# A one-layer streaming encoder: natural projections in 512-column stripes, weights in a ring, tokens in half pieces

## The chip, the core and the metric

The kernel runs on one core of one Trainium2 chip. The metric is the device time of one execution in microseconds. The core has a matrix engine (TensorE, PE in the profile, with its weight loads as PEld), VectorE (DVE), ScalarE (ACT), GpSimd (POOL) and SyncE (SP), whose queue issues all of this kernel's transfers. Each engine works through its own queue in order; semaphores join them.

## The reference, cut to what matters

One layer over 16 meta tokens and 2048 prompt tokens, and over 8 streams of 16 new tokens, in float32. All projections of a layer are columns of one weight matrix `w_in` of 1024 x 8280:

```
h  = layer_norm(tokens)
(g_q, g_k, g_v, g_low, g_r, d_q, d_k, d_v, i_q, i_k, i_w, d_z, m_a, m_b) = split(h @ w_in)
A) log_f = log_sigmoid(g_low @ gla_w2 + b) / 16 ; S_t = diag(exp(log_f)) S_{t-1} + k^T v ; o = q S
   y_a = (rms_norm(o) * g * silu(g_r)) @ w_gla                       # linear attention, 4 heads
B) I[t,s] = sum_h w[t,h] relu(q_idx[t,h] . k_idx[s]) ; keep the best 256 keys of each token
   y_b = (softmax attention over the kept keys * silu(d_z)) @ w_dsa  # 16 heads, 4 key heads
out = layer_norm(ALPHA * h + (sigmoid(m_a + .) * y_a + sigmoid(m_b + .) * y_b) @ w_out)
```

New keys, values, indexer keys and recurrence states are returned too.

## The kernel before, in words

A matrix product in float32 is made of three: each operand is split into a high part and the rest, and `mm3` (L265 to L267) multiplies high by high, high by low and low by high, for eight blocks k of 128 rows, 24 matmuls in all, into one PSUM tile.

The 17 tiles of 128 tokens and the 16 meta tokens form six pieces of up to 384 columns. `phase_keys` normalizes each tile, transposes it into x (`xh`, `xl`, 8 blocks by 384 columns each) and computes keys, values and the indexer's keys from two sets of 300 weight columns. Then `project(g)` runs for three groups of two pieces: [4, 5], [2, 3], [0, 1]. The x of the first group stays from `phase_keys`; that of the others is read back from `d_xt` and split again. A stripe is a set of weight columns: `weights` loads it from `w_in` in pieces (`raw`), ScalarE casts each to its high part `whi`, GpSimd subtracts for `wlo` (L144). A transposed stripe (`stripe_t`, `tsp`) has the weights stationary and passes 272 or 384 token columns; a natural stripe (`natural`, `nat`) has 128 tokens stationary and passes the weights. gv, gr and z are natural, in 256 columns. Results are evicted through tiles of the pool `ev` and stored to scratch in DRAM.

Between the stripes of a group stand the indexer's blocks (`index_block`: scores, relu on ScalarE, weighted sum on VectorE), and `select`, a search on VectorE for each token's threshold that makes the masks of the kept keys. It is put 2500 instructions later than written, so that it runs beside the projections.

`phase2` runs the attention `attend(j)` for j from 15 down. Between its steps stands the side work: the gates of the linear attention (`gla_gates`), the sample streams' attention, their linear attention, then 16 chunks. 13 steps of it are put 1500 instructions earlier than written, so that they can run beside the last projections. The output projections follow (`gla_project`, `finish`).

The order on every engine is written out by a scheduler that simulates the program when it is built: of the instructions that are ready it takes the one written first, moved by the shifts above. A tile takes a place of its pool, and waits until the tile that had that place, or that had the same bytes in an earlier pool, is read for the last time. Pools lie on a stack from the left and one from the right. From the left stand, in `phase1`, after a constant: kp, scp, iqp, tk, jk, then xp0, xp1, xp2 (24 KB a partition each), ev, ws. In `phase2` stand there kdu0, kdu1, stu, gi, gt, gm, gc, sb. The side work's large tiles are in sb: three places under the tag `s4`, of 4.25 KB, and two of `kn`, of 2 KB. A chunk of the gates has two tiles `x` and two `e` there. Three x pools are handed out by the list `slots`; the last group has xp2 and xp1. In the last stripe of the second group the pieces are taken in reverse (`flip`).

Lines used below: L144 `tt`, L156 `act`, L159 the cast in `split_sb`, L256 the weight DMAs, L445 and L446 the indexer's matmuls, L596 the x loads, L611 the natural stores, L682 the gates' matmul, L1192 the sample attention's scores, L1129 to L1133 attention's scores and maxima.

Of the kernel before, what the change touches and what calls it, by code (L numbers as in the profile page):

```python
# [21 lines left out]
P = 128  # L22
# [31 lines left out]
VLATE = 60  # L54
PIECE = 720
# [64 lines left out]
class Trunk:  # L120
    def __init__(self, tc, i, o):
        self.tc, self.nc, self.i, self.o = tc, tc.nc, i, o
        self.turn = 0
        self.spare = self.flip = False
# [115 lines left out]
    def weights(self, parts, pool=None, name="", eng=None):  # L240

        nc = self.nc
        width = sum(n for _, n in parts)
        w = self.i["w_in"][0].rearrange("(k p) c -> p k c", p=P)
        if pool is None:
            hi = self.ws.tile([P, KT, width], F32R, name="whi")
            lo = self.ws.tile([P, KT, width], F32R, name="wlo")
        else:
            hi = pool.tile([P, KT, width], F32R, name="whi" + name, tag="sc")
            lo = pool.tile([P, KT, width], F32R, name="wlo" + name, tag="sc")  # L250
# [23 lines left out]
    def prep_x(self, t, xh, xl, c, keep):  # L274
# [9 lines left out]
        for q in range(2):  # L284
            ps = self.pi.tile([P, 4, P], F32, name="pt", tag="pi")
            for k in range(4):
                kk = 4 * q + k
                nc.tensor.transpose(ps[:, k, :r], h[:r, kk * P : (kk + 1) * P], self.ident[:r, :r])
            s = slice(4 * q, 4 * q + 4)
            self.split(xh[:, s, c : c + r], xl[:, s, c : c + r], ps[:, :, :r])  # L290
            if keep is not None:
                f = self.ev.tile([P, 4, P], F32, name="xf", tag="ev")
                nc.scalar.copy(f[:, :, :r], ps[:, :, :r])
                nc.sync.dma_start(keep[:, s, c : c + r], f[:, :, :r])

    def nat(self, x, c, r, w):

        ps = self.pp.tile([P, 512], F32, name="pp")
        (hi, lo), (xh, xl) = w, x
        n = hi.shape[-1]  # L300
        self.mm3(ps[:r, :n], lambda k: xh[:, k, c : c + r], lambda k: xl[:, k, c : c + r],
                 lambda k: hi[:, k, :], lambda k: lo[:, k, :], KT)
        return ps[:r, :n]

    def tsp(self, x, c, n, w, a):

        ps = self.pp.tile([P, 512], F32, name="pp")
        (hi, lo), (xh, xl) = w, x
        self.mm3(ps[:, :n], lambda k: hi[:, k, a : a + P], lambda k: lo[:, k, a : a + P],
                 lambda k: xh[:, k, c : c + n], lambda k: xl[:, k, c : c + n], KT)  # L310
        return ps[:, :n]

    def keys(self, t, x, c, w1, w2):
# [13 lines left out]
        xi = self.ev.tile([P, 80], F32, name="xi", tag="evs", bufs=4)  # L327
# [16 lines left out]
        xd = self.ev.tile([P, 2, 64], F32, name="xd", tag="evs", bufs=4)  # L344
# [8 lines left out]
        gl = self.ev.tile([16, P], F32, name="gl", tag="evs", bufs=4)  # L353
# [32 lines left out]
    def xtiles(self):  # L386
        q = self.slots.pop(0)
        return [self.xp[q].tile([P, KT, PMAX], F32R, name="x" + n) for n in "hl"]

    def stripe_t(self, g, c0, width, meta, evac):  # L390
        w = self.weights([(c0, width)])
        for q in GROUPS[g][:: -1 if self.flip else 1]:
# [167 lines left out]
    def phase1(self):  # L560
        nc, tc, i = self.nc, self.tc, self.i
        with ExitStack() as c:
# [7 lines left out]
            self.xp = [c.enter_context(tc.tile_pool(name=f"xp{q}", bufs=1)) for q in range(3)]  # L570
            self.ev = c.enter_context(tc.tile_pool(name="ev", bufs=4))
# [8 lines left out]
            self.x, self.slots = {}, [0, 1, 2, 0, 1, 2, 0, 1, 2, 1]  # L580
# [7 lines left out]
    def project(self, g):  # L588
        nc = self.nc
        for q in GROUPS[g]:  # L590
            if q not in self.x:
                self.x[q] = xh, xl = self.xtiles()
                n = PCN[q]
                for k in range(0, KT, 2):
                    raw = self.raw(n)
                    nc.sync.dma_start(raw, self.d["xt"][q][:, k : k + 2, :])  # L596
                    self.split_sb(xh[:, k : k + 2, :n], xl[:, k : k + 2, :n], raw)
# [4 lines left out]
        def natural(col, dst, base, meta, evac):  # L602
            w = self.weights([(col, 256)])
            for t, q in tiles:
# [5 lines left out]
                evac(e[:r, :256], ps)  # L610
                nc.sync.dma_start(self.d[dst][COL[t] : COL[t] + r, col - base : col - base + 256], e[:r, :256])  # L611
# [4 lines left out]
        def silu_norm(e, ps):  # L616
            self.act(e, ps, AF.Silu)
            self.tt(e, e, self.gng[:], OP.mult, eng=nc.gpsimd)
# [5 lines left out]
            "gv": (4, lambda c: natural(C_GV + c, "gv", C_GV, True, self.copy)),  # L624
            "q": (4, lambda c: st(g, C_DQ + c, 256, False, self.ev_heads)),
            "gr": (4, lambda c: natural(C_GR + c, "gr", C_GR, False, silu_norm)),
            "z": (4, lambda c: natural(C_DZ + c, "z", C_DZ, False, silu)),
# [4 lines left out]
        def step(n, c):  # L632

            self.spare = g == len(GROUPS) - 1 and n in SPARE

            self.flip = g == len(GROUPS) - 2 and (n, c) == (order[-1], 256 * (kinds[n][0] - 1))
            kinds[n][1](c)
            self.spare = self.flip = False

        steps = [lambda n=n, c=256 * q: step(n, c) for n in order for q in range(kinds[n][0])]  # L640
# [849 lines left out]
```

## Time and profile before

| | us |
|---|---|
| median of 3 runs (3590.15 to 3598.61) | 3597.57 |
| the profiled execution's own time | 3593.96 |
| its span | 3592.2 |
| TensorE busy | 3483.6 |
| VectorE busy | 2528.4 |
| ScalarE busy | 1450.9 |
| GpSimd busy | 1088.8 |

Busy times are sums over the whole span, which has stages with different limits: keys to about 200 us, projections to about 1860 us, attention with side work, and the output stage from about 3190 us. A matmul's recorded time runs until its last column is out and covers part of the next matmul's; how dense TensorE works is seen from the times between starts, or from the weight loads.

### The profile page before, as it was taken

To read this page: it belongs to the slowest core of one execution; us is meant where nothing else is said; L and a number is where in the kernel's file an instruction comes from. 1 tells how busy PE (TensorE), PEld (TensorE's weight loads), DVE (VectorE), ACT (ScalarE), POOL (GpSimd) and SP (SyncE) were. 2 spreads that over 40 slices of the span, in tenths; PEclk is the share of its full clock that TensorE was granted. 3 is DMA by queue.
4 is the path that set the end of the run, shared out by engine and by line. 5 is a ranking of instruction groups with operands and counts; after the bars stand their busy time and mean duration, and the time that the engine had idled before them with its cause. 6 is when DMAs were issued, how large, how long until landed. Compare 5 with 4: busy or idle time off the path is not lost. (4 is left out here: it accounts for less than half of the span.)

```text
span 3592.2 us, 66024 instructions
## 1 busy us (share of the span) xinstructions
PE 3483.6 (97%) x24196; PEld 3212.5 (89%) x24196; DVE 2528.4 (70%) x5813; ACT 1450.9 (40%) x3092; POOL 1088.8 (30%) x1412
## 2 busy tenths in 40 slices
PE   7999999999999998999999999999999999989999
PEld 6999999999999998998887788888877888879998
DVE  7737998799999998964436677676765666544444
ACT  4435223433324323322535556566565344331110
POOL 3122242242342334434411345455410000022221
PEclk9999999999999999999999999999999999999999
DMA  8642443254442345445573433333343345564431
GB/s 265 202 131 82 139 121 108 83 157 127 119 145 73 103 134 148 140 134 159 171 199 94 122 109 97 102 105 99 100 121 88 89 120 135 151 192 136 124 115 62
DMA packets 550340, 457.77 MB, mean 127 GB/s; under 512 B 95248, under 2 KB 522528, under 8 KB 550016
## 3 DMA queue, kind: packets, MB, share of 16 engines
q1 hardware_dynamic: 550016, 453.56, 43.9%
q8 instruction: 190, 3.11, 0.4%
q14 instruction: 134, 1.10, 0.1%
HBM read 292.49 MB, written 160.92 MB: 126 GB/s over the span
## 5 line engine op out<-in xcount | busy, mean ns | idle before, releaser
L144 POOL TENSOR_TENSOR wlo<-raw,whi 128x512 fp32r<-128x512 f32 x360 | 482.3, 1360 | 817.1 <-ACT whi L159 706.7
L150 DVE TENSOR_SCALAR_CACHE_REDUCE junk<-sc,cand 128x272 bf16<-128x272 f32 (+6 forms) x512 | 701.6, 1370 | 16.9
L265 PE MATMUL pp<-whi,xh 128*128 128x256 f32 (+3 forms) x1952 | 562.1, 288 | 3.5 <-ACT whi L159 2.3
L265 PE MATMUL pp<-xh,whi 128*128 128x384 f32 (+2 forms) x1728 | 563.6, 326 | 1.9 <-ACT whi L159 1.1
L267 PE MATMUL pp<-whi,xl 128*128 128x256 f32 (+3 forms) x1952 | 560.8, 288 | 4.4 <-DVE xl L144 4.4
L267 PE MATMUL pp<-xh,wlo 128*128 128x384 f32 (+2 forms) x1728 | 563.0, 327 | 1.0 <-POOL wlo L144 1.0
L266 PE MATMUL pp<-xl,whi 128*128 128x384 f32 (+2 forms) x1728 | 563.4, 326 | 0.0
L266 PE MATMUL pp<-wlo,xh 128*128 128x256 f32 (+3 forms) x1952 | 561.9, 288 | 0.0
L265 PEld LDWEIGHTS pp<-whi,xh 128*128 128x128 f32 (+1 forms) x1952 | 371.9, 191 | 12.7 <-issue 4.3
L267 PEld LDWEIGHTS pp<-whi,xl 128*128 128x128 f32 (+1 forms) x1952 | 371.0, 190 | 11.3 <-DVE xl L144 6.9
L266 PEld LDWEIGHTS pp<-wlo,xh 128*128 128x128 f32 (+1 forms) x1952 | 371.5, 190 | 7.8 <-issue 5.2
L1131 DVE CUSTOM_DVE_ANT_0 lgl<-pl,mkl 128x348 f32<-128x348 f32 (+8 forms) x608 | 296.1, 510 | 102.8 <-PE pl L1130 65.8
L265 PE MATMUL pd<-xh,wh 128*128 128x242 f32 (+3 forms) x1152 | 327.7, 285 | 8.2 <-ACT wh L1347 4.5
L159 ACT CAST whi<-raw 128x512 fp32r<-128x512 f32 (+1 forms) x344 | 199.2, 622 | 319.7 <-DMA raw<-in_w_in 204.8
L265 PEld LDWEIGHTS pp<-xh,whi 128*128 128x128 f32 x1728 | 325.1, 188 | 3.3 <-ACT whi L159 1.7
L267 PEld LDWEIGHTS pp<-xh,wlo 128*128 128x128 f32 x1728 | 324.8, 188 | 2.5 <-POOL wlo L144 1.8
L266 PE MATMUL pd<-xl,wh 128*128 128x242 f32 (+3 forms) x1152 | 324.6, 282 | 2.1 <-DVE xl L144 2.1
L266 PEld LDWEIGHTS pp<-xl,whi 128*128 128x128 f32 x1728 | 325.1, 188 | 0.6
L267 PE MATMUL pd<-xh,wl 128*128 128x242 f32 (+3 forms) x1152 | 324.5, 282 | 0.8 <-POOL wl L144 0.8
L156 ACT ACTIVATE lgl<-lgl,mx 128x1040 f32<-128x1040 f32 (+7 forms) x256 | 249.9, 976 | 177.9 <-DVE mx L1133 171.4
L1129 PE MATMUL pl<-kd,q 128*128 128x348 f32 (+14 forms) x800 | 302.5, 381 | 14.1 <-DVE mx L1131 4.9
L1130 PE MATMUL pl<-kd,q 128*128 128x348 f32 (+14 forms) x800 | 261.7, 330 | 0.0
(252 smaller groups left out, 7592.7 us busy)
## 6 DMA issues: line engine op xcount, KB each, us to landing
raw<-in_w_in SPq DMA_DIRECT2D x360, 256.0 KB, 3.2
q<-d_q SPq DMA_DIRECT2D x272, 128.0 KB, 3.0
d_h<-x SPq DMA_DIRECT2D x17, 512.0 KB, 3.3
d_gv<-en SPq DMA_DIRECT2D x68, 128.0 KB, 1.9
d_gr<-en SPq DMA_DIRECT2D x68, 128.0 KB, 2.0
d_z<-en SPq DMA_DIRECT2D x68, 128.0 KB, 1.7
v<-d_gv SPq DMA_DIRECT2D x17, 512.0 KB, 3.7
gr<-d_gr SPq DMA_DIRECT2D x17, 512.0 KB, 3.6
```

The costliest lines, as they stand in the source:

```text
L144: (eng or self.nc.vector).tensor_tensor(out, a, b, op=op)
L150: (eng or self.nc.vector).tensor_scalar(out, a, s1, s2, op0=op0, op1=op1, **kw)
L156: self.nc.scalar.activation(out, a, f, **kw)
L159: (self.nc.vector.tensor_copy if self.spare else self.nc.scalar.copy)(out, src)
L265: mm(ps, ah(k), bh(k), start=k == 0, stop=False)
L266: mm(ps, ah(k), bl(k), start=False, stop=False)
L267: mm(ps, al(k), bh(k), start=False, stop=k == n - 1)
L1129: nc.tensor.matmul(ps[:, :m], q[:, u, :], kd, start=True, stop=False)
L1130: nc.tensor.matmul(ps[:, :m], q[:, 2 + u, :], kd, start=False, stop=True)
L1131: nc.vector.tensor_tensor_reduce(lg[z1][:, a : a + m], ps[:, :m], mk[z1][:, a : a + m], 1.0, NEG, OP.add, OP.max, mx[:, s : s + 1])
```

## The change

Natural stripes have 512 columns. The weight tiles `whi` and `wlo` of 8 blocks become rings of six places each, every place 1024 elements a partition: four blocks of a 256-column stripe or two of a 512-column one; `weights` now returns two functions of k. Raw pieces hold two blocks up to 384 columns and one of 512, in four places instead of three. x is kept in halves of four blocks, each half in one of five pools taken in turn, and `slots` and `flip` are gone. The pool ev has six places instead of four, its small tiles eight instead of four. The area that the program reserves for dynamic DMAs at the foot of every partition is 1 KB instead of 16 KB.

```diff
+DMA_SCRATCH = 1024
+RING = 6
+RAWB = 4
...
     def raw(self, n):
-        t = self.ws.tile([P, 2 * PMAX], F32, name="raw", bufs=3)
-        return t[:, : 2 * n].rearrange("p (k c) -> p k c", k=2)
+        t = self.ws.tile([P, 2 * PMAX], F32, name="raw", bufs=RAWB)
+        two = 2 if n <= PMAX else 1
+        return t[:, : two * n].rearrange("p (k c) -> p k c", k=two)
...
     def weights(self, parts, pool=None, name="", eng=None):
...
-        if pool is None:
-            hi = self.ws.tile([P, KT, width], F32R, name="whi")
-            lo = self.ws.tile([P, KT, width], F32R, name="wlo")
...
-        for q in range(4):
-            s = slice(2 * q, 2 * q + 2)
-            raw = self.raw(width)
-            a = 0
-            for c, n in parts:
-                nc.sync.dma_start(raw[:, :, a : a + n], w[:, s, c : c + n])
-                a += n
-            self.split_sb(hi[:, s, :], lo[:, s, :], raw, eng)
-        return hi, lo
+        each = 1024 // width if pool is None else KT
+        hi, lo = [], []
+        for q in range(0, KT, each):
+            for x, name in (hi, "whi"), (lo, "wlo"):
+                if pool is None:
+                    t = self.ws.tile([P, 1024], F32R, name=name, bufs=RING)
+                    x.append(t[:].rearrange("p (k c) -> p k c", c=width))
+                else:
+                    x.append(pool.tile([P, KT, width], F32R, name=name + str(width), tag="sc"))
+            two = 2 if 2 * width <= 2 * PMAX else 1
+            for k in range(0, each, two):
+                raw = self.raw(width)[:, :two]
+                a = 0
+                for c, n in parts:
+                    nc.sync.dma_start(raw[:, :, a : a + n], w[:, q + k : q + k + two, c : c + n])
+                    a += n
+                self.split_sb(hi[-1][:, k : k + two, :], lo[-1][:, k : k + two, :], raw, eng)
+        return (lambda k: hi[k // each][:, k % each, :]), (lambda k: lo[k // each][:, k % each, :]), width
...
     def xtiles(self):
-        q = self.slots.pop(0)
-        return [self.xp[q].tile([P, KT, PMAX], F32R, name="x" + n) for n in "hl"]
+
+        halves = []
+        for _ in range(2):
+            self.xp.append(self.xp.pop(0))
+            halves.append([self.xp[-1].tile([P, 4, PMAX], F32R, name="x" + n) for n in "hl"])
+        return list(zip(*halves))
...
-            self.xp = [c.enter_context(tc.tile_pool(name=f"xp{q}", bufs=1)) for q in range(3)]
-            self.ev = c.enter_context(tc.tile_pool(name="ev", bufs=4))
+            self.xp = [c.enter_context(tc.tile_pool(name=f"xp{q}", bufs=1)) for q in range(5)]
+            self.ev = c.enter_context(tc.tile_pool(name="ev", bufs=6))
...
         def natural(col, dst, base, meta, evac):
-            w = self.weights([(col, 256)])
+            w = self.weights([(col, 512)])
...
                 e = self.ev.tile([P, 512], F32, name="en", tag="ev")
-                evac(e[:r, :256], ps)
-                nc.sync.dma_start(self.d[dst][COL[t] : COL[t] + r, col - base : col - base + 256], e[:r, :256])
+                evac(e[:r], ps)
+                nc.sync.dma_start(self.d[dst][COL[t] : COL[t] + r, col - base : col - base + 512], e[:r])
...
-            "gv": (4, lambda c: natural(C_GV + c, "gv", C_GV, True, self.copy)),
+            "gv": (2, lambda c: natural(C_GV + c, "gv", C_GV, True, self.copy)),
...
-            self.flip = g == len(GROUPS) - 2 and (n, c) == (order[-1], 256 * (kinds[n][0] - 1))
...
-    nc = bacc.Bacc("TRN2", target_bir_lowering=False, num_devices=1)
+    nc = bacc.Bacc("TRN2", target_bir_lowering=False, num_devices=1, dynamic_dma_scratch_size=DMA_SCRATCH)
```

gr and z go from four stripes to two in the same way.

## Rows read from the trace of the kernel before

**Rows 1.** The page, parts 1 and 2: busy us of TensorE; its granted clock by slice.

```profile
PE 3483.6 (97%) x24196; PEld 3212.5 (89%) x24196; DVE 2528.4 (70%) x5813; ACT 1450.9 (40%) x3092; POOL 1088.8 (30%) x1412
PEclk9999999999999999999999999999999999999999
```

**Rows 2.** Windows: stretch, length, busy us (xinstructions) by engine, clock, DMA share, GB/s.

```profile
core 0: us, PE busy (x) PEld busy (x) DVE busy (x) ACT busy (x) POOL busy (x), PEclk, DMA share, GB/s
0.00:200.00 200.00, 175.73 (x1231) 168.06 (x1231) 140.15 (x301) 83.92 (x245) 48.61 (x52) 0.98 0.72 218
200.00:1600.00 1400.00, 1379.50 (x9380) 1368.35 (x9380) 1235.02 (x1984) 502.61 (x1040) 484.02 (x402) 1.00 0.42 121
1600.00:1860.00 260.00, 254.99 (x1719) 234.36 (x1718) 100.14 (x197) 101.34 (x163) 91.62 (x63) 0.98 0.60 171
1860.00:2640.00 780.00, 757.28 (x5198) 625.94 (x5200) 535.60 (x1894) 455.35 (x976) 330.35 (x642) 0.99 0.39 107
2640.00:3190.00 550.00, 526.20 (x4171) 459.78 (x4165) 330.80 (x1109) 246.36 (x540) 46.10 (x160) 0.99 0.45 121
3190.00:3592.20 402.20, 389.85 (x2505) 356.06 (x2505) 186.68 (x330) 61.34 (x129) 88.07 (x95) 0.99 0.40 124
```

**Rows 3.** Timeline of TensorE, 499 to 509 us: two of 80 matmuls, 76 starts apart.

```profile
499.93 0.28 PE L265 MATMUL pp<-whi,xh 128*128 128x256 f32 x1
509.05 0.28 PE L266 MATMUL pp<-wlo,xh 128*128 128x256 f32 x1
```

**Rows 4.** Timeline of TensorE, output stage: two of 44 matmuls, 42 starts apart.

```profile
3573.94 0.39 PE L265 MATMUL fo<-woh,mgh 128*128 128x512 f32 x1
3583.46 0.39 PE L265 MATMUL fo<-woh,mgh 128*128 128x512 f32 x1
```

**Rows 5.** Tile whi on TensorE: min/median/max ns, first and last start us.

```profile
L265 PE MATMUL pp<-whi,xh x1952: 274/283/617, 13.5 to 1749.5; 128*128 128x256 f32 x163, 128*128 128x300 f32 x28, 128*16 128x256 f32 x4, 128*16 128x300 f32 x1
L266 PE MATMUL pp<-xl,whi x1728: 276/334/522, 179.5 to 1858.5; 128*128 128x384 f32 x161, 128*128 128x256 f32 x28, 128*128 128x272 f32 x3
```

**Rows 6.** Groups by shape, 200 to 1860 us, ScalarE and GpSimd: count, busy, mean ns, idle before.

```profile
L159 ACT CAST whi<-raw 128x512 fp32r<-128x512 f32 x325 | 187.0, 620 | 302.5 <-DMA raw<-in_w_in 191.4 <-PE pp L266 108.5 <-issue 1.7
L144 POOL TENSOR_TENSOR wlo<-raw,whi 128x512 fp32r<-128x512 f32 x351 | 469.4, 1357 | 789.0 <-ACT whi L159 678.5 <-DVE whi L159 20.2 <-PE pi L446 18.9
L144 POOL TENSOR_TENSOR xl<-raw,xh 128x768 fp32r<-128x768 f32 x12 | 21.9, 1848 | 25.6 <-ACT xh L159 25.6
```

**Rows 7.** Waits of TensorE, 100 to 1860 us: us, times, longest.

```profile
PE pi L445 <- ACT rl L156: 18.8, 14, 4.2
PE pp L265 <- ACT whi L159: 1.1, 2, 0.6
```

**Rows 8.** The page, part 3: DMA queues, packets, MB, share.

```profile
q1 hardware_dynamic: 550016, 453.56, 43.9%
q8 instruction: 190, 3.11, 0.4%
q14 instruction: 134, 1.10, 0.1%
```

**Rows 9.** Tile d_xt: loads of x pieces, us from issue to landing.

```profile
DMA to landing us min/median/max: 2.5/3.7/4.9
```

**Rows 10.** Windows of tile pg alone (TensorE, its loads, VectorE, ScalarE).

```profile
1600.00:1860.00 260.00, 46.19 (x202) 26.70 (x202) 26.09 (x48) 22.86 (x43) 0.98 0.60 171
```

**Rows 11.** Windows of tile ge alone (VectorE, ScalarE, GpSimd).

```profile
1600.00:1860.00 260.00, 27.96 (x24) 31.04 (x40) 20.56 (x10) 0.98 0.60 171
```

**Rows 12.** Groups of ScalarE, 1600 to 1860 us.

```profile
L156 ACT ACT_TABLE_LOAD x21 | 26.9, 1283 | 0.4
```

**Rows 13.** Tiles gl and ks on TensorE: first and last start us.

```profile
L682 PE MATMUL pg<-gl,w x40: 374/587/692, 1673.3 to 1747.3; 16*128 16x512 f32 x24, 16*128 16x400 f32 x8, 16*128 16x256 f32 x8
L1192 PE MATMUL pg<-ks,qsh x32: 282/287/428, 1757.7 to 1918.2; 128*128 128x272 f32 x32
```

More of the change, by code (lines that the diff above doesn't have):

```diff
@@ L123, in __init__ @@
         self.turn = 0
-        self.spare = self.flip = False
+        self.spare = False
     @contextmanager
@@ L289, in prep_x @@
             s = slice(4 * q, 4 * q + 4)
-            self.split(xh[:, s, c : c + r], xl[:, s, c : c + r], ps[:, :, :r])
+            self.split(xh[q][:, :, c : c + r], xl[q][:, :, c : c + r], ps[:, :, :r])
             if keep is not None:
@@ L326, in keys @@
         nc.sync.dma_start(d["v"][c0 : c0 + r, :], vt[:r])
-        xi = self.ev.tile([P, 80], F32, name="xi", tag="evs", bufs=4)
+        xi = self.ev.tile([P, 80], F32, name="xi", tag="evs", bufs=8)
         nc.scalar.copy(xi[:r, 0:64], p2[:, 212:276])
@@ L343, in keys @@
         self.stt(xi[:r, 0:64], xi[:r, 0:64], mu, self.ing[:r], OP.subtract, OP.mult)
-        xd = self.ev.tile([P, 2, 64], F32, name="xd", tag="evs", bufs=4)
+        xd = self.ev.tile([P, 2, 64], F32, name="xd", tag="evs", bufs=8)
         for q in range(2):
@@ L352, in keys @@
         self.split(self.kih[:, kc : kc + r], self.kil[:, kc : kc + r], ps[:, 0, :r])
-        gl = self.ev.tile([16, P], F32, name="gl", tag="evs", bufs=4)
+        gl = self.ev.tile([16, P], F32, name="gl", tag="evs", bufs=8)
         nc.scalar.copy(gl[:, :r], ps[:16, 1, :r])
@@ L386, in xtiles @@
     def xtiles(self):
-        q = self.slots.pop(0)
-        return [self.xp[q].tile([P, KT, PMAX], F32R, name="x" + n) for n in "hl"]
+        halves = []
[3 more added lines that the diff above has]
+        return list(zip(*halves))
     def stripe_t(self, g, c0, width, meta, evac):
         w = self.weights([(c0, width)])
-        for q in GROUPS[g][:: -1 if self.flip else 1]:
+        for q in GROUPS[g]:
             s = META if q == 0 and not meta else 0
@@ L596, in project @@
                     nc.sync.dma_start(raw, self.d["xt"][q][:, k : k + 2, :])
-                    self.split_sb(xh[:, k : k + 2, :n], xl[:, k : k + 2, :n], raw)
+                    r = slice(k % 4, k % 4 + 2)
+                    self.split_sb(xh[k // 4][:, r, :n], xl[k // 4][:, r, :n], raw)
         tiles = [(t, q) for q in GROUPS[g] for t in PIECES[q]]
@@ L623, in project @@
             "gk": (2, lambda c: st(g, C_GK + c, 256, True, self.ev_act("gk", C_GK, AF.Copy))),
[L624 removed]
+            "gv": (2, lambda c: natural(C_GV + c, "gv", C_GV, True, self.copy)),
             "q": (4, lambda c: st(g, C_DQ + c, 256, False, self.ev_heads)),
[L626 to L627 removed]
+            "gr": (2, lambda c: natural(C_GR + c, "gr", C_GR, False, silu_norm)),
+            "z": (2, lambda c: natural(C_DZ + c, "z", C_DZ, False, silu)),
             "ma": (4, lambda c: st(g, C_MA + c, 256, False, self.ev_act("ma", C_MA, AF.Sigmoid, biascol=0))),
@@ L634, in step @@
             self.spare = g == len(GROUPS) - 1 and n in SPARE
-            self.flip = g == len(GROUPS) - 2 and (n, c) == (order[-1], 256 * (kinds[n][0] - 1))
             kinds[n][1](c)
-            self.spare = self.flip = False
-        steps = [lambda n=n, c=256 * q: step(n, c) for n in order for q in range(kinds[n][0])]
+            self.spare = False
+        wide = "gv", "gr", "z"
+        steps = [lambda n=n, c=(512 if n in wide else 256) * q: step(n, c) for n in order for q in range(kinds[n][0])]
         blocks = [t for t, _ in tiles if t not in ("m", "s", 0)]
```

20 lines of the change are left out of this document (8 added, 12 removed).

## The prediction

> **What bounds the kernel now.** I read the page's busy times first, then TensorE's busy time by stretches, then who TensorE waits for, then single matmuls. TensorE is busy for 97% of the span at a clock near full speed [rows 1]; but a matmul's recorded time covers part of the next one, so I look at its weight loads as well. From 200 to 1600 us they fill 1368 of 1400 us, while VectorE fills 1235, ScalarE 503 and GpSimd 484 [rows 2]: the projections are bound by TensorE. From 1860 to 2640 us (attention, with the linear-attention side work between) the loads fill 626 of 780 us and no engine is full [rows 2]: that stretch has holes. In 3190 to 3592 us TensorE is dense again. Inside the projections TensorE waits little: 18.8 us for the indexer's relu, about 1 us for weights [rows 7]. So what an edit takes from TensorE before 1858.5 us, where the last projection matmul starts [rows 5], should come off the end, unless something else becomes late.
>
> **The change, part by part.**
>
> *Wide stripes.* The natural projections gv, gr and z give every row tile its x block as the stationary operand and pass the weights through. The trace holds 1952 such matmuls for each of three lines [rows 5]; 36 calls of keys (18 tiles, two halves) make 288 of each, which leaves 1664, and three lines make 4992 matmuls of 256 columns. They become 2496 of 512. In the unbroken stretch shown, 76 matmuls of 256 columns start within 9.12 us, 120 ns each [rows 3]. The output stage has the 512-column form, with the same kinds of operands: 42 start within 9.52 us, 227 ns each [rows 4]. Two old ones take 240 ns, one new one 227: 13 ns saved, times 2496 is 32.4 us. Rounding in the view leaves both means good to about 0.3 ns, so 31 to 34 us. I take 32.
>
> The Trainium skill ("TensorE: Matmul & The Clock Gate", Back-to-back issue gap) gives columns/2.4 GHz plus about 2.5 ns between warm matmuls. By that a pair costs 218.3 ns against 215.8, and the sum would be 6 us instead of 32. The trace differs: both forms stand some 13 ns above columns/2.4 [rows 3, 4], so I go by the rows.
>
> *Evictions, stores, gate product.* Their number halves: the same bytes leave in half as many instructions on ScalarE, GpSimd and SP. ScalarE and GpSimd are busy a third of the projections [rows 2], TensorE does not wait for these evictions [rows 7], so 0. If that cover were gone, the smaller instruction counts would still only help. More eviction buffers: they can end waits of ScalarE and VectorE for stores, none of which reaches TensorE in the rows; 0, and at most the 18.8 us of the relu wait as a gain.
>
> *The ring.* A narrow stripe fills two of six places for its high parts and two for its low, so three fit; before there were two. A wide stripe needs four, so of a wide stripe that follows a wide one only the first half (k 0 to 3) can be split ahead. The second half waits until the last tile has read k 0 and 1, which is 18 of its 24 matmuls before the end (18 x 0.227 = 4.1 us), and is wanted 12 matmuls (2.7 us) into the next stripe: 6.8 us in all. The raw piece can already lie in one of four raw places. Then one k takes a ScalarE cast of 0.62 us and a GpSimd subtraction of 1.36 us [rows 6]; the place with k 4 and 5 is ready after 0.62 + 2 x 1.36 = 3.3 us, and k 6 and 7 follow at the same pace. That hides. If the raw piece must first be fetched, 3.7 us (the landing of such pieces [rows 9]) make it 7.0 us: 0.2 us late. There are four such joints in a group, twelve in all; bounds 0 and, with another GpSimd or ScalarE instruction ahead at each, some 2 us a joint, 24 us. I take 0, nearest to the rows: TensorE waited for a split for 1 us in all.
>
> *Halves of x.* Five half places instead of three whole ones. At a change of group one half is loaded ahead; the next two come free when the last stripe leaves its first piece, one only with that stripe's end. A half needs two raw pieces: landing 3.7 us, then two subtractions of 1.85 us [rows 6, 9], 7.4 us. The cover is the first piece's two column blocks, 48 matmuls of at least 120 ns [rows 3], 5.8 us, plus the first half of the next piece. Bounds 0 and 7.4 us at two joints, 15 us; I take 2 us in all.
>
> *Selection behind the projections.* VectorE is 88% busy from 200 to 1600 us [rows 2]. If TensorE reaches the last group some 20 us earlier and VectorE does not, the indexer's wait of 18.8 us grows. Bounds 0 and 20 us; I take 3 us, since other stripes stand in the queue between.
>
> *The smaller dynamic-DMA area.* Every issue in the trace is on the hardware queue or an instruction fetch [rows 8]; nothing uses the area. 0. But the left stack now begins 15 KB lower, and this moves what lies on what.
>
> *Side work that loses its place.* The gates of the linear attention (first matmul 1673.3, last 1747.3 us) and the sample attention (from 1757.7 us) run beside the last projections [rows 13]. Their pool sb begins, by the tile sizes, 82.5 KB above the stack's first pool and is 16.8 KB long. The x pools begin 77 KB above it. Before, the first x pool, 24 KB, holds all of sb, and the last group has left it. After, pools of 12 KB: sb lies in pools 0 and 1, and the turn gives the last group pools 1 to 4. Two of sb's three large places then wait for the last stripe to leave the first piece, and the gates need three. I expect the gates only some 10 us before the projections end. Between 1600 and 1860 us the matmuls of pg, the side work's, are busy 46 us [rows 10]: the projections end 46 us earlier than the saving alone makes it, and these 46 us go into the stretch with the holes. There gates also bring ScalarE 31 us and VectorE 28 us [rows 11], and 27 us of table loads [rows 12]. Bounds for what that stretch grows by: 0 (all in holes) and 112 us (84 us from the first gate to the first sample matmul [rows 13], with ScalarE held by the gates so that attention's exponentials wait, and the 27 us of table loads once more). I take 46, as if TensorE's work were moved at its price: net 0.
>
> **Sum.** -32 + 2 + 3 + 0 = -27 us on the profiled execution's own 3594.0 us (a span of 3592.2 and 1.8 around it). The median of the runs is 3597.6, 3.6 above; the same difference gives 3570.
>
> **Rivals.**
> 1. *Side work fills the holes.* It finds them in 1860 to 2640 us, where the weight loads leave 154 us [rows 2]. Then the 46 us come off too: 3570 - 46 = 3524. For it: no engine is full there. Against: chains through four engines, whose work is not simply stacked.
> 2. *Side work holds attention up.* The stretch grows by the 112 us above: 3570 - 46 + 112 = 3636. For it: gates and attention both need ScalarE, with different tables. Against: attention can put scores and transposes between. It decides for slower once the stretch grows by more than 46 + 27 + 11 = 84 us.
> 3. *The ring is too short for wide stripes.* 24 us at the twelve joints: 3594. For it: GpSimd's splits wait on ScalarE, which serves evictions in the same queue. Against: weights have cost TensorE 1 us so far [rows 7].
> 4. *A wide matmul saves nearly nothing.* If the 13 ns belonged to the narrow form's weight loads, each new one would cost two old ones less 2.5 ns, and 26 us of the sum would be gone: 3596. Against: the 512-column row itself [rows 4]. The formula of the Trainium skill cited above comes to the same.
>
> **How the numbers follow.** My forecast 0.56, rival 1 0.15, rival 2 0.14, rival 3 0.10, rival 4 0.05. A measurement here tells about 0.3%, 11 us, from no change: faster is below 3587, slower above 3608. The forecast and rival 1 are faster, 0.71; rivals 3 and 4 the same, 0.15; rival 2 slower, 0.14. The range reaches into rival 1 (half of it lies above 3530) and past rivals 3 and 4 with their small terms at the upper bounds: 3530 to 3604. The forecast's own range is 3548 to 3586, with the side work's net between -22 and +16.
>
> **What would show it.** Right: 1664 - 832 matmuls a line, 512 columns at 227 ns; the last projection matmul near 1780 us; the first gate near 1770 us, no longer near 1673; TensorE's waits for weights before that still a few us. The side work's last chunk later against attention than before, and the output stage starting some 27 us earlier. Wrong: gates that still begin among the projections by 100 us (my reading of the memory is false; then the projections end near 1830 us), weight waits of tens of us (rival 3), a stretch from the projections' end to the output stage longer than before by over 84 us (rival 2) or shorter than before (rival 1).

## The result and the profile after

The changed kernel takes 3630.78 us, median of 4 runs (3623.54 to 3634.68), against 3594.98 us (4 runs too, 3590.15 to 3598.61) for the kernel before on the same chip: a ratio of 1.0099, 95% interval [1.0081, 1.0117]. It is slower by 36 us where 27 us less were forecast. The profiled execution took 3623.54 us (span 3621.7), 29.6 us more than the profiled one of before; the stage numbers below compare these two.

Part 1 of the page after: TensorE has 2496 matmuls fewer than before [rows 1], as counted.

```profile
PE 3473.6 (96%) x21700; PEld 3080.2 (85%) x21700; DVE 2520.9 (70%) x5801; ACT 1442.9 (40%) x3000; POOL 1076.9 (30%) x1378
PEclk9999999999999999999979999999999999999999
```

One digit of the clock has dropped to 7: the slice from 1811 to 1901 us. The timeline of TensorE after shows a wide stripe: the first and the last of 57 matmuls without a gap, so 56 starts in 12.69 us, 226.6 ns each.

```profile
494.76 0.39 PE L276 MATMUL pp<-whi,xl 128*128 128x512 f32 x1
507.45 0.39 PE L275 MATMUL pp<-wlo,xh 128*128 128x512 f32 x1
```

That is the 227 ns of the output stage [rows 4] against two of 120 [rows 3]: the wide matmul does what was priced. Now the windows after (stretch, length, busy us of TensorE, loads, VectorE, ScalarE, GpSimd, granted clock, DMA share, GB/s), against [rows 2]:

```profile
200.00:1600.00 1400.00, 1374.90 (x7298) 1269.45 (x7297) 1236.77 (x1986) 499.15 (x951) 479.22 (x371) 1.00 0.41 122
1600.00:1860.00 260.00, 225.59 (x1183) 186.75 (x1181) 78.14 (x158) 79.91 (x116) 70.15 (x53) 0.89 0.47 142
1860.00:2640.00 780.00, 759.17 (x5237) 620.63 (x5238) 531.85 (x1891) 469.93 (x1002) 294.46 (x576) 0.99 0.39 104
2640.00:3190.00 550.00, 526.52 (x4098) 458.98 (x4097) 333.01 (x1119) 238.13 (x537) 85.11 (x223) 0.99 0.46 122
```

Fewer loads from 200 to 1600 us are no loss: each load now serves more columns. In 1600 to 1860 us TensorE is busy 226 us where it was 255, at a clock of 0.89 where it was 0.98. The lines of single tiles after say what moved (count, min/median/max ns, first and last start): the last projection matmul, the gates, the sample attention, the stores of the linear attention's outputs, and the output projections.

```profile
L275 PE MATMUL pp<-xl,whi x1728: 278/334/522, 172.4 to 1795.9; 128*128 128x384 f32 x161, 128*128 128x256 f32 x28, 128*128 128x272 f32 x3
...
L694 PE MATMUL pg<-gl,w x40: 374/626/1217, 1639.7 to 1875.6; 16*128 16x512 f32 x24, 16*128 16x400 f32 x8, 16*128 16x256 f32 x8
...
L1204 PE MATMUL pg<-ks,qsl x32: 283/288/291, 1882.9 to 2027.4; 128*128 128x272 f32 x32
...
L863 SPq DMA_DIRECT2D d_oa<-ot x17: 359/371/557, 2139.5 to 2746.2; - x17
...
L274 PE MATMUL pd<-xh,wh x1152: 218/278/582, 2786.0 to 3581.2; 128*128 128x242 f32 x86, 128*128 128x256 f32 x86, 128*128 128x240 f32 x10, 128*128 128x128 f32 x10
```

The last two of these lines in the kernel before:

```profile
L851 SPq DMA_DIRECT2D d_oa<-ot x17: 360/371/558, 2032.6 to 2634.4; - x17
...
L265 PE MATMUL pd<-xh,wh x1152: 218/278/580, 2673.0 to 3552.0; 128*128 128x242 f32 x86, 128*128 128x256 f32 x86, 128*128 128x240 f32 x10, 128*128 128x128 f32 x10
```

The projections end 62.6 us earlier (1795.9 against 1858.5 [rows 5]). But of the gates' 40 matmuls only four start at 1639.7; the others start from 1789.4 to 1875.6, where all 40 stood from 1673 to 1747 before [rows 13]:

```profile
1789.37 0.93 PE L694 MATMUL pg<-gl,w 16*128 16x400 f32 x2
```

So everything behind them in the side work is late: the first output of the linear attention by 107 us, the last by 112, the first output projection by 113.

Where TensorE then stands idle, by windows of 20 us after (same columns):

```profile
1780.00:1800.00 20.00, 18.36 (x106) 15.22 (x104) 7.25 (x16) 15.17 (x20) 3.76 (x2) 1.00 0.55 172
1800.00:1820.00 20.00, 5.85 (x7) 2.19 (x8) 7.21 (x10) 10.14 (x11) 2.71 (x2) 0.51 0.87 283
1820.00:1840.00 20.00, 13.71 (x37) 8.15 (x37) 13.81 (x35) 13.96 (x16) 4.76 (x3) 0.67 0.68 196
1840.00:1860.00 20.00, 17.10 (x66) 10.67 (x64) 14.15 (x36) 18.21 (x27) 5.61 (x5) 0.80 0.27 93
1860.00:1880.00 20.00, 16.16 (x91) 11.41 (x92) 12.56 (x33) 18.15 (x28) 5.00 (x4) 0.88 0.35 121
1880.00:1900.00 20.00, 19.88 (x142) 16.79 (x141) 14.90 (x51) 14.50 (x29) 1.73 (x3) 0.95 0.35 80
```

Right behind the projections TensorE does 7 matmuls in 20 us, and the granted clock is 0.51, near the lower level of 1.2 GHz; it reaches 0.95 only 80 us later. ScalarE is busy up to 18 of 20 us there: of its 60 us from 1800 to 1880, the gates' activations are 23 and table loads 19, the rest is mostly attention's. TensorE's waits after, 100 to 1860 us (us, times, longest):

```profile
PE pi L456 <- ACT rl L159: 22.2, 18, 3.6
PE pg L694 <- DVE gx L153: 15.8, 2, 9.9
PE pg L694 <- DMA raw<-in_w_in: 9.4, 1, 9.4
...
PE pp L276 <- POOL wlo L147: 2.1, 2, 1.7
...
PE pp L274 <- ACT whi L162: 0.4, 1, 0.4
```

The gates' product (L694) waits for places and for its input, 25 us in three waits. The weights cost TensorE 2.1 us and 0.4 us: the ring holds.

Two tables that I worked out from all starts go through the rest. The first holds times in the span (us), each the first or last start of the tile's line (the gates of after without the four early matmuls): the side work as a chain.

```
kernel        projections  gates  first    last     first output  TensorE
              end          from   d_oa     d_oa     projection    ends
before        1858.7       1673   2032.6   2634.4   2673.0        3584.3
after         1796.1       1789   2139.5   2746.2   2786.0        3613.6
e2            1817.2       1812   2170.2   2767.8   2806.3        3625.3
e1            1845.3       1639   1994.4   2592.6   2776.6        3610.4
e7            1850.1       1666   2025.9   2627.3   2763.4        3592.9
e6            1848.5       1643   1999.0   2597.2   2640.9        3589.9
e16           1815.6       1654   2007.9   2604.9   2643.5        3562.2
e19           1842.4       1664   2009.3   2612.5   2648.5        3577.1
```

The second splits TensorE's time from start to start: up to columns/2.4 GHz + 14 ns (the rows' own 120 and 227 ns; at least 109, the median for 128 columns) counts as work, what is over as lost. "Head" is from the start of the third group of projections to the first d_oa, "middle" from there to the output stage.

```
kernel        work     lost: groups 1, 2   head    middle   all
before        3133.6         17.0          109.0   278.2    438.1
after         3107.5         28.1          166.4   272.0    493.7
e2            3136.2         20.9          154.5   273.3    476.1
e1            3104.7         27.8          118.4   313.8    492.9
e7            3135.1         15.8          104.0   296.5    445.1
e6            3103.0         30.8          120.5   299.0    474.2
e16           3101.9         24.0          118.3   281.8    447.6
e19           3131.4         17.0          103.4   285.8    433.0
```

So the wide stripes saved 26 us of work, and 56 us of holes came, 57 in the head and 11 in groups 1 and 2, with a few less elsewhere. The head ends with the chain, so a late chain also makes it longer. The windows from the end of the projections to the first d_oa show what that means, before and after:

```profile
1858.70:2032.60 173.90, 160.60 (x1005) 121.50 (x1004) 112.78 (x358) 86.48 (x174) 24.95 (x50) 0.97 0.46 129
1796.10:2139.50 343.40, 302.66 (x1883) 226.13 (x1881) 219.65 (x687) 209.33 (x382) 48.33 (x74) 0.93 0.44 122
```

The stretch is hardly sparser (weight loads for 70% of it before, 66% after), but it is twice as long; by the count of the second table 60.7 us are lost in it before and 133.6 after. (Labels of experiments are cut to their number; what each changes is told next.)

### The profile page after: what moved, and what is told of

Its sections match the earlier page's. It is cut to its first block, busy times and chain, and to the rows that moved or that the text cites. A ratio compares the mean times of both kernels' runs of the same rounds, so it can differ in the third digit from the quotient of the medians.

```text
span 3621.7 us, 60614 instructions
## 1 busy us (share of the span) xinstructions
PE 3473.6 (96%) x21700; PEld 3080.2 (85%) x21700; DVE 2520.9 (70%) x5801; ACT 1442.9 (40%) x3000; POOL 1076.9 (30%) x1378
## 5 line engine op out<-in xcount | busy, mean ns | idle before, releaser
L276 PE MATMUL pp<-whi,xl 128*128 128x512 f32 (+3 forms) x1120 | 414.8, 372 | 3.5 <-DVE xl L147 3.5
L275 PE MATMUL pp<-wlo,xh 128*128 128x512 f32 (+3 forms) x1120 | 414.7, 371 | 0.0
L274 PE MATMUL pp<-whi,xh 128*128 128x512 f32 (+3 forms) x1120 | 413.3, 372 | 1.2 <-ACT xh L162 0.8
L156 DVE SCALAR_TENSOR_TENSOR sc<-rl,iw,sc 128x388 f32<-128x388 f32 (+16 forms) x308 | 215.4, 735 | 82.1 <-ACT rl L159 80.9
L1101 PE MATMUL oo<-pt,v 128*64 128x256 f32 x1088 | 258.8, 386 | 3.3 <-ACT pt L1085 2.4
L1077 PE MATMUL px<-ident,lgl 128*128 128x128 f32 x1600 | 248.2, 276 | 13.1 <-ACT lgl L159 5.2
```

The costliest lines, as they stand in the source:

```text
L156: self.nc.vector.scalar_tensor_tensor(out, a, s, b, op0=op0, op1=op1)
L274: mm(ps, ah(k), bh(k), start=k == 0, stop=False)
L275: mm(ps, ah(k), bl(k), start=False, stop=False)
L276: mm(ps, al(k), bh(k), start=False, stop=k == n - 1)
L1077: nc.tensor.transpose(ps[:, 2 * s + u, :], pe[u][a // KLOW][:, a % KLOW : a % KLOW + P], self.ident[:])
L1101: self.nc.tensor.matmul(oo[0][64 * o : 64 * o + 64, k : k + 2, :], self.v[:, s0 + s, d : d + 64], t[:, 2 * s : 2 * s + 2], start=self.fres ...
```

## The experiments: where the side work lies

By the addresses of the two programs sb lay wholly inside xp0 before, a pool that the last group had left; after, it lies across xp0 and xp1, and xp1 is one that the last group still reads. In both programs sb begins 5.6 KB above the first x pool: the smaller DMA area moved the two alike, and it is the pools of half the size, with their turn, that put sb on a busy one. The experiments undo this, do it alone, and take its consequences one by one. Times are medians, each ratio against the kernel before in the same series.

**e1**: sb below the busy pools, by taking the pool stu after it.

```diff
-            self.stu = left("stu")
 ...
             self.sb = left("sb")
+            self.stu = left("stu")
```

> The changed kernel, with the pool stu (12 KB, attention's alone) moved from the third place of the left stack of phase 2 to the last, behind sb. sb then lies from 71 to 87.5 KB above the stack's first pool, inside the free x pool 0 and what is below it; stu lies on the busy x pool 1. Theory A (the side work lost its place in memory): the gates start beside the projections again, by about 1690 us, the last projection matmul is near 1825 us, and the time falls by the 27 us of the sum below the kernel before: 3560 to 3575 us. Theory B (the wider stripes, the ring or another order of the instructions cost the time, and the late gates only go with it): no change against the changed kernel, 3620 to 3635 us.

3616.98 us, 1.0070 [1.0053, 1.0087], between the two expectations. The gates are back at 1639 us and the side work's last output comes at 2593, earlier than before; but the output projections start at 2776.6, as late as after:

```profile
L863 SPq DMA_DIRECT2D d_oa<-ot x17: 359/376/1658, 1994.4 to 2592.6; - x17
...
L274 PE MATMUL pd<-xh,wh x1152: 218/278/583, 2776.6 to 3578.0; 128*128 128x242 f32 x86, 128*128 128x256 f32 x86, 128*128 128x240 f32 x10, 128*128 128x128 f32 x10
```

Now stu lies on the pool of the output projections' weights. The holes left the head (118 us) and stand in the middle (314): attention runs without the output projections between its steps.

**e2**: the kernel before, with nothing but another turn of its three x pools, so that the last group holds the one that sb lies in.

```diff
-            self.x, self.slots = {}, [0, 1, 2, 0, 1, 2, 0, 1, 2, 1]
+            self.x, self.slots = {}, [2, 1, 0, 2, 1, 0, 2, 1, 0, 1]
```

> The kernel before, with the x pools 0 and 2 exchanged in the list of turns and nothing else: the last group now has pools 0 and 1, and sb lies in pool 0, which its first piece holds to the last stripe. Theory A: the gates wait for the end of the projections, about 1830 us here, the side work's last chunk is stored some 110 us later than in the kernel before, and the time rises by what the changed kernel lost beyond its saving, about 56 us: 3640 to 3660 us. Theory B: as the kernel before, 3590 to 3600 us.

3628.04 us, 1.0106 [1.0091, 1.0121], less than the 3640 expected at least: this alone makes the kernel before as slow as the changed one. Its gates and output projections:

```profile
L682 PE MATMUL pg<-gl,w x40: 374/587/1056, 1812.0 to 1907.0; 16*128 16x512 f32 x24, 16*128 16x400 f32 x8, 16*128 16x256 f32 x8
...
L265 PE MATMUL pd<-xh,wh x1152: 218/278/579, 2806.3 to 3592.9; 128*128 128x242 f32 x86, 128*128 128x256 f32 x86, 128*128 128x240 f32 x10, 128*128 128x128 f32 x10
```

Work is that of before; 38 us are lost more, 45.5 more in the head and none in the middle.

**e3**: after, with gv, gr and z back in 256 columns (six edits like this one).

```diff
-            w = self.weights([(col, 512)])
+            w = self.weights([(col, 256)])
```

> The changed kernel with gv, gr and z in 256 columns again (ring, half pools, buffers and the small area kept). If a wide matmul saves the 13 ns that two starts show, TensorE has 32 us more work and the projections end 32 us later, near 1828 us: 3655 to 3665 us. If the wide stripes are themselves part of the loss (joints of the ring), less than that or even a gain: 3610 to 3640 us.

3624.72 us, 1.0095 [1.0080, 1.0110]. The loss stays without wide stripes: pools, ring and buffers bring it. TensorE's work is 3135.5 us, 28.0 above the wide form's, and yet the kernel is no slower than with them.

**e5**: after, with no side work ahead of attention.

```diff
-NEARLY = 13
+NEARLY = 0
```

> The changed kernel with no step of the side work moved ahead (NEARLY 0 instead of 13), so that attention stands first in the order at the projections' end and the gates come between its steps. If the loss is the hole behind the projections, in which gates hold ScalarE and attention waits (1790 to 1900 us, some 30 us more lost than before): 3590 to 3615 us. If the loss is that the side work ends 112 us later and the output projections with it: the same or slower, 3630 to 3680 us.

3624.08 us, 1.0091 [1.0076, 1.0106], between the two expectations. The edit did less than it was to: the gates start at 1781, right behind the projections, three of their products still stand ahead of attention, and attention's first score comes 24 us behind the projections' end (after: 30). The output projections start at 2786.7, as after. So e5 alone does not decide whether attention held up by the gates, the way in which my rival 2 put it, is what costs. Attention's first score after, in e2 and in e16 (told below) says more:

```profile
1826.20 0.63 PE L1141 MATMUL pl<-kd,q 128*128 128x348 f32 x1 [4.50 <-DMA q<-d_q]
1823.81 0.63 PE L1129 MATMUL pl<-kd,q 128*128 128x348 f32 x1 [4.76 <-DMA kd<-d_kd]
1850.33 0.49 PE L1141 MATMUL pl<-kd,q 128*128 128x348 f32 x1
```

In e2, as slow as after, it comes 7 us behind the projections' end; in e16, the fastest, 35 us. A late start of attention is not what makes the difference; whether ScalarE slows attention further on is not separated.

**e6** and **e8**: stu on the right stack, over a pool that is needed late; sb as low as in e1. e6 keeps the wide stripes, e8 has the edits of e3 too.

```diff
-            self.stu = left("stu")
 ...
+            self.stu = inner.enter_context(tc.tile_pool(name="stu", bufs=1, side="right"))
```

> The changed kernel with the pool stu taken from the left stack and put on the right stack beside up. sb lies 10 KB lower, inside the free x pool 0 and below, as in the run before that moved stu to the left stack's end; but stu now lies where later only the last merge buffer stands, not on the weights of the output projections. Theory C (the end follows the start of the output projections, which need the side work's end and the memory of their weights): gates by 1700 us, side work ended near 2595 us, first output-projection matmul near 2635 us instead of 2777 to 2786, time 3550 to 3580 us. Theory D (the projections gained little because VectorE's selection holds them, and attention takes as long as it takes): 3590 to 3615 us.

> The same with gv, gr and z in 256 columns. Theory T (TensorE bounds the projections, a wide matmul saves 13 ns): the last projection matmul 32 us later and the time 25 to 35 us above the run with wide stripes. Theory D (VectorE's selection bounds part of the projections and the static order gives the rest back): the last projection matmul at most 10 us later, the time within 10 us.

e6: 3594.12 us, 1.0011 [1.0002, 1.0020]. e8: 3588.18 us, 0.9994 [0.9984, 1.0005]. The output projections of e6 start at 2640.9 us:

```profile
L274 PE MATMUL pd<-xh,wh x1152: 218/280/511, 2640.9 to 3557.6; 128*128 128x242 f32 x86, 128*128 128x256 f32 x86, 128*128 128x240 f32 x10, 128*128 128x128 f32 x10
```

The place of sb and stu gives most of the loss back (from 1.0099 to 1.0011 of the kernel before, some 32 us; 37 by the medians, which are of two series), and no more: the 3550 to 3580 us of theory C did not come. With it mended, wide stripes are still not faster than narrow ones: 28 us less work, 40 us more holes, 34 of them between 200 us and the projections' end, which comes at 1848.5 in e6 and at 1842.1 in e8.

**e7**: the kernel before with the edit of e1, to price the late output projections alone.

> The kernel before, with one edit: the side work's pool stu is taken behind sb instead of ahead of it. No stripe, ring or shift is changed. By the tile sizes sb then lies 12 KB lower and stu lies on the output projections' weights. Theory M (a late start of the output projections costs by itself, whatever the stripes are): the gates stay near 1640 to 1675 us, the side work ends near 2590 to 2630 us, yet the first output projection starts near 2750 to 2790 us instead of 2673, and the time rises by 15 to 35 us: 3605 to 3625. Rival W (the late start cost something only because the wide stripes had made the stages before it sparse): the start moves as said but the time stays within 10 us of the kernel before. Rival N (the pools' order does not hold the output projections): their start stays within 15 us of 2673.

3600.34 us, 1.0030 [1.0019, 1.0040]. They start at 2763.4 us, 90 us late, and it costs 12 us, less than the 15 to 35 expected: 18 us more are lost in the middle. At this price the late output projections of e2 (133 us late) would be the smaller part of its 37 us, and e2 has no more holes in the middle than the kernel before; the larger part is the long head. Why the same edit shows 36 us in the middle of e1 I have not found out.

## The experiments: what becomes of the wide stripes' saving

**e9** and **e10**: e6 and e8 with half the steps of the threshold search (`select` leaves out the finer thresholds, so other keys are kept). It frees VectorE.

```diff
-        for b in range(30, -1, -1):
+        for b in range(30, 14, -1):
```

> As the kernel with stu on the right and wide stripes, but each threshold search does 16 steps of its 31 (the thresholds are coarser: part of the computation is left out). VectorE has some 300 us less to do in the projections. Theory D: the indexer's waits of TensorE (22 us in the changed kernel) go to a few us and the projections end earlier by 10 to 20 us than with the full search. Theory T: no change of the projections' end beyond 3 us.

> The same short search with 256-column stripes. Theory D: with VectorE out of the way the last projection matmul is 25 to 35 us later than with wide stripes and the short search, the full 13 ns a matmul. Theory T: the same difference as between the two kernels with the full search, whatever that is.

One run each: 3592.16 us wide, 3601.60 narrow (before: 3589.40). The wait for the relu goes (22.9 us in e6, none in e9; 14.5 in e8, 2.9 in e10), but other waits come, above all of 11 and 12 us for a load of cached keys, and e9 gains 2 us while e10 loses 13. Wide is 9 us ahead here, by single runs, and its projections end 7 us earlier (1840.1 against 1846.7), not the 25 to 35 of theory D. An uncertain answer: taking work from VectorE changes the order everywhere.

**e11, e12, e13**: e6 with the shifts scaled down, both or one. The instructions of a group of projections fell to 0.83 of their number, and a shift counts instructions.

```diff
-SEL_LATER = 2500
+SEL_LATER = 2000
 ...
-EARLY = 1500
+EARLY = 1200
```

> The changed kernel with stu on the right stack, and the two shifts of the order that are counted in instructions made smaller in the proportion in which the wide stripes made a group shorter (5351 instructions instead of 6444, 0.83): select 2000 instead of 2500 instructions later, the early side work 1200 instead of 1500 earlier. Theory P (the shifts kept their count, so selection came later and the gates earlier in time; that is why the 28 us of TensorE's work came back as waits for the indexer's relu and for the gates' loads): those waits (22.9 and 8.6 us) go back to the 14.5 and 0 of the narrow kernel or below, and the time is 3560 to 3578 us. Theory Q (the wide stripes are coarse units that the written order always fits worse): 3588 to 3600 us as with the shifts unscaled.

> Only select scaled, 2000 instead of 2500. Theory P: the indexer's waits go back, the gates' wait of 8.6 us stays: 3570 to 3585 us. Theory Q: 3588 to 3600 us.

> Only the early side work scaled, 1200 instead of 1500. Theory P: the gates' wait of 8.6 us goes, the indexer's stay: 3578 to 3590 us. Theory Q: 3588 to 3600 us.

Both: 3580.05 us, 0.9974 [0.9962, 0.9985]. SEL_LATER alone: 3593.76, 1.0013 [1.0004, 1.0022]. EARLY alone: 3581.76, 0.9980 [0.9972, 0.9989]. All of it is EARLY; the wait for the relu stays (22.4, 22.5 and 22.5 us), so theory P fails for the selection. In e6 TensorE's waits, 200 to 1800 us, begin with

```profile
PE pi L456 <- ACT rl L159: 22.9, 18, 3.6
PE pg L694 <- issue: 8.6, 1, 8.6
```

The gates' first product holds up for 8.6 us the matmuls behind it in TensorE's queue, which could have run: in e6 and in the changed kernel (last section) they are matmuls of a stripe already begun. The view names no cause here and a load of `raw` in the changed kernel, but in both the product starts just when its own weights land: in the changed kernel they are issued at 1635.2 us and land after 4.3, in e6 their load is issued 2 us before the product:

```profile
L988 SPq DMA_DIRECT2D w<-in_gla_w x1: 343/343/343, 1640.7 to 1640.7; - x1
DMA to landing us min/median/max: 1.7/1.7/1.7
```

With 1200 the product stands later in the queue, the load has long landed (issued at 1637.5), and the wait is gone: the gates start at 1662 instead of 1643, and the projections end at 1824 instead of 1849.

**e14**: the mirror, e8 with both shifts up by 1.25 (SEL_LATER 3125, EARLY 1875).

> The mirror: the kernel with 256-column stripes and stu on the right, with both shifts 1.25 times as large (3125 and 1875). Theory P: narrow stripes now get the waits that the wide ones had, 15 to 30 us more than the 3588 us with the shifts as they were: 3600 to 3620 us. Theory Q: 3583 to 3593 us, no change.

3593.89 us, 1.0018 [1.0008, 1.0027]: worse by 6 to 9 us (medians, ratios), just above what theory Q expected. The waits that theory P expected did not come (14.4 us for the relu, 0.4 for the gates' product).

**e15**: e13 with `EARLY = 900`. **e18**: the narrow e8 with `EARLY = 1200`.

> Wide stripes, stu on the right, EARLY 900 where 1200 gave 3581 and 1500 gave 3594. Theory S (the shift counts instructions, and wide stripes have 0.83 of the old count, so 1250 is the old place): 1200 is near the best, and 900 puts the gates later, first gate near 1680 us or behind, with their matmuls nearer the projections' end; time 3578 to 3592, not below 3576. Rival G (any smaller shift is better, whatever the count): another 8 to 14 us less, 3566 to 3573.

> Narrow stripes in the new pools, stu on the right, EARLY 1200 (with 1500 it was 3588). Theory S (the shift's meaning scales with the count of instructions): the narrow form's place was right at 1500, so 1200 brings nothing or costs: 3585 to 3595; wide at 1200 (3581) stays 5 us or more below. Rival G (a smaller shift is better with any stripes): 8 to 14 us less, 3574 to 3580, and then the wide stripes bring nothing at the end at all.

e15: 3579.65 us, 0.9971 [0.9960, 0.9982], the same as with 1200. e18: 3610.12 us, 1.0052 [1.0038, 1.0066], 22 us worse than narrow with 1500. So the gain of the smaller shift belongs to the wide stripes, as far as these values show. e18 lies above its expected range; the shift acts in jumps, and that 0.83 is the rule behind it was not shown.

**e16**: e13 with one more relu buffer. **e19**: the same buffer in e8.

```diff
-        r = self.ev.tile([P, 512], F32, name="rl", bufs=3)
+        r = self.ev.tile([P, 512], F32, name="rl", bufs=4)
```

> Wide stripes, stu on the right, EARLY 1200, and four buffers instead of three for the indexer's relu tile rl. Theory R (part of the wide stripes' saving is lost in TensorE's wait for the indexer's relu, 22 us from 200 to 1800 us, because the relu waits for a buffer): that wait falls by 5 to 15 us and the time falls by as much, 3567 to 3576. Rival Q (the relu waits for VectorE's queue behind the search, not for a buffer): the wait stays within 3 us of 22 and the time within 4 us of 3581.

> Narrow stripes in the new pools, stu on the right, EARLY 1500 (their better shift), and four buffers for rl. Theory R (the relu's buffer is short because the wide stripes' long matmuls leave the indexer fewer places to be fitted in): the narrow form gains at most 3 us from it, 3585 to 3590, and wide stripes at their best (3573) stay 12 us or more below. Rival Q2 (the buffer helps any stripes alike): the narrow form gains 7 to 11 us, 3577 to 3581, and wide at their best stay only 4 to 8 us below.

e16: 3572.97 us, 0.9950 [0.9938, 0.9963]; e19: 3587.16, 1.0000 [0.9991, 1.0009]. The relu wait, 200 to 1800 us, in e13 and then in e16:

```profile
PE pi L456 <- ACT rl L159: 22.5, 16, 3.6
```

```profile
PE pi L456 <- ACT rl L159: 17.8, 13, 4.2
```

The wait falls by 4.7 us (a little under the 5 to 15 expected), the time by 9; the narrow form gains nothing (0.9994 in e8, 1.0000 here). e16 is the best version: 0.5% below the kernel before, where the changed one is 1.0% above. Each form at the best of what was tried for it, wide stripes are worth 14 us by the medians (3572.97 against 3587.16, two series) and 18 by the ratios. By the second table they have 29.5 us less work there and 14.6 us more holes, 14.9 of them in the head: the projections end 27 us earlier, the gates start only 10 earlier, and the difference is time behind the projections with too little to do.

## Why the prediction was wrong, point by point

- **Side work that loses its place**: this step failed. I saw rightly that sb comes to lie on a busy pool and when the gates would start (10 us ahead of the projections' end; all but four matmuls start from 1789.4, 7 us ahead of it). I then priced the move at the 46 us of TensorE time of the moved matmuls [rows 10], net 0. What moved was a chain with a length of its own. In the first table the first d_oa comes 345 to 360 us after the gates begin in every kernel (before 359, after 350, e2 358, e6 356, e16 354; over all runs 335 to 367), the last another 597 to 607 us later, and the output projections 36 to 44 us after that, unless something else blocks them. Before, 185 of the 359 us lay beside dense projections; after, 7 of the 350. The projections' end came 62.6 us earlier instead of 78 and the stretch from there to the output stage grew by 91 us instead of 46 (its first matmul is at 3188.3 before and 3216.5 after, so 1329.6 and 1420.4 us). By the count of the second table 24 us of this growth are matmuls that moved and 67 are holes. TensorE's end moved by these and the output stage's 1 us: -62.6 + 90.8 + 1.1 = +29.3. e2 shows the cause alone, e6 takes it away.
- **Rival 2** had the right place and nearly the right price (3636; its own mark was a growth of over 84 us), and the chance of 0.14 was too low. Its mechanism was half right: the side work holds the stage up, but by its own length with nothing dense beside its head, and not by a late start of attention (e2 against e16). My upper bound of 112 us [rows 12, 13] held, though the table loads in it did not double: 21 from the gates to the first d_oa before and after. I took a value near the middle though the nearest row, the 84 us of the gates' span, was a chain's length and not TensorE's busy time.
- **Wide stripes, -32**: nearly right in size: 226.6 ns a matmul, and 26 to 30 us less work in every pair. The Trainium skill ("TensorE: Matmul & The Clock Gate", Back-to-back issue gap) gives columns/2.4 GHz plus 2.5 ns as the gap of an isolated matmul. By that formula the estimate would have been 6 us; the trace disagrees with it for these forms, of which each loads a new stationary operand, and measures 13 ns above columns/2.4 GHz. What failed was the sentence that this comes off the end: with the side work mended, 0 came (e6 against e8), and 14 to 18 after two other edits (e16 against e19).
- **Selection behind the projections, +3 (0 to 20)**: low. The relu wait grew only from 18.8 [rows 7] to 22.2 us, but the holes of groups 1 and 2 grew by 11 us. A fourth relu buffer takes part of it back (e16), so the wait is partly one for a buffer.
- **Ring 0, halves of x +2, evictions 0**: right. Weights cost 2.5 us of waits in all, xl 0.5. Rival 3 is refuted, and so is rival 4 by the 226.6 ns. Rival 1 (holes filled, 3524) is refuted by the head.
- **Small DMA area 0**: nothing shows a price of its own. I wrote that it moves what lies on what; among the pools of the left stack it does not, since it moves all of them by the same 15 KB. The five half pools moved sb onto a busy one.

Open: the 36 us in the middle of e1, and whether the gates can start as much earlier as the projections now end.

## What to carry to other kernels

When an edit moves memory, list which early work lies on whose bytes, and price moved work as a chain from its first instruction to its first output, with what runs beside it, not as the busy time of its instructions on the bottleneck engine. Work taken out of a dense stage reaches the end only if what follows the stage can start earlier by as much: look for the chain that begins inside the stage. And when instructions become fewer, try the orders that are written as counts of instructions again: here that and one buffer turned nothing into 14 to 18 us.

## What the runs showed of the hardware

Behind a wait of 9.4 us TensorE ran at half its speed. In the timeline of TensorE after, around the gates' early product (start, us, in brackets the idle time before it):

```profile
1629.92 0.40 PE L275 MATMUL pp<-wlo,xh 128*16 128x512 f32 x1
1639.74 3.00 PE L694 MATMUL pg<-gl,w 16*128 16x400 f32 x4 [9.42 <-DMA raw<-in_w_in]
1642.67 0.61 PE L276 MATMUL pp<-whi,xl 128*16 128x512 f32 x1
...
1645.63 0.63 PE L274 MATMUL pp<-whi,xh 128*16 128x512 f32 x1
1646.06 0.63 PE L275 MATMUL pp<-wlo,xh 128*16 128x512 f32 x1
...
1647.03 0.39 PE L275 MATMUL pp<-wlo,xh 128*16 128x512 f32 x1
1647.26 0.40 PE L276 MATMUL pp<-whi,xl 128*16 128x512 f32 x1
```

Behind the wait 512 columns take 430 ns from start to start (columns/1.2 GHz is 427), from 1647 us on 230 again. In the windows of 10 and 5 us the clock is 1.00, then 0.65 and 0.50, then 0.83:

```profile
1620.00:1630.00 10.00, 10.00 (x63) 9.70 (x61) 3.16 (x6) 0.00 (x0) 3.03 (x3) 1.00 0.69 207
1630.00:1640.00 10.00, 0.58 (x3) 0.29 (x2) 3.88 (x12) 0.00 (x0) 2.52 (x2) 0.65 0.74 213
1640.00:1645.00 5.00, 5.00 (x10) 1.70 (x10) 0.88 (x3) 0.00 (x0) 2.48 (x2) 0.50 0.64 188
1645.00:1650.00 5.00, 5.00 (x19) 2.18 (x18) 0.22 (x1) 0.00 (x0) 0.00 (x0) 0.83 0.03 13
```

With dense matmuls behind it, this cost some ten slow ones, 2 us, and the product itself, whose four matmuls take 3.00 us here and 1.60 in e5 at 1781 us. In the head, where the work is sparse, the clock stayed below 0.9 for 80 us: a hole there also makes the work in it slower.
